# Filler matmuls moved ahead of a query sum and into the attention, in a one-core decoder layer on Trainium2

## The chip, the cores and the metric

The kernel runs on one core of a Trainium2 chip. The metric is the device time of one execution in microseconds (us). The engines have the names that the profile gives them: PE (TensorE) multiplies matrices, PEld is its loading of weights, DVE (VectorE), ACT (ScalarE) and POOL (GpSimd) work on tiles of 128 partitions, and SP (SyncE) here only issues DMA transfers.

## The reference

One layer of a hybrid decoder on 512 rows of 1024 numbers, all in float32:

```python
h = h + 0.5 * _swiglu(h, ffn1_norm, ffn1_w_gate, ffn1_w_up, ffn1_w_down)   # D_FF = 2816
h = h + _mixing(h, ...)
h = h + 0.5 * _swiglu(h, ffn2_norm, ffn2_w_gate, ffn2_w_up, ffn2_w_down)

def _mixing(x, ...):
    proj = _rmsnorm(x, mix_norm) @ w_in       # q, 6 x k/v, nsa_gate, ssm_u, gate_nsa, gate_ssm
    ...
    y_nsa = o_nsa @ w_nsa_proj    # 8 heads of 64: compressed, selected and window attention, gated and summed
    y_ssm = _s5_glu(...)          # a state space over 512 steps, GELU, then val * sigmoid(gate)
    merged = jax.nn.sigmoid(gate_nsa) * y_nsa + jax.nn.sigmoid(gate_ssm) * y_ssm
    return merged @ w_out
```

With 512 rows the selection and the window take in every earlier row, so these two branches are causal attention with keys of their own.

## The kernel before

Values lie transposed: a tile is 128 features by 512 rows. A product in float32 is made of three faster ones: both operands are split into a rounded high part and a remainder (`whi`, `wlo`; `xgh`, `xgl`), and `mm3` (L371 to L374) issues high by high, low by high and high by low. Weights come through SP's queue, in order, as slabs of 512 KB (eight blocks of 128 x 128, so 24 matmuls of 512 columns). There are five raw slabs; for each, ACT writes `whi` (L233) and DVE `wlo` (L234) two slabs ahead of use, into three slots. Other tiles come from one heap of 58 tiles of 256 KB (`H`), and the results of PE from eight banks (`PS`).

The order of the work on PE is written out by hand; the orders on the other engines come from a scheduler that follows it. The stages:

- The first feed-forward (until about 384 us). In its shadow the tables of the state space are prepared (`s5_prep`): 16 heap tiles, `vr`, `vi`, `er` and `ei` for four groups, which stay in the heap until each is used.
- The mixing's projections. `M1_ORDER` lists them: `u`, the compressed keys and values, the four state-space steps `S` (`s5_state`, first matmul L1058) and outputs `Y`, and the queries `q`. A query tile is squared by ACT (`qsq`, L1285), and `q_sums` (L1310) sums the squares on PE; the sums of tile t stand behind query tile t+1, and those of tile 3 stand alone. `q_scale` makes the scales `qs` of them. `cmp_k_norm` makes the compressed keys: ACT (`k2c`, `k2ct`), then DVE, which spreads them into the two `k2z` tiles (L1250, L1252), read by `c_scores` (`cs`, L1386).
- The attention: 64 units of a head, a branch and a quarter t of the rows. A unit is scored (`scores`, on DVE and ACT a softmax of (t+1) x 128 columns, tile `P`), turned by transposes two units later (`turn`, `pt`, L1457), and weighed (`weigh`). Between these PE does filler (`filler`): the projections of the 16 gate columns listed in `FILL` (`gs` and `gn`, tile `fx`) and the products of the state space's gated unit (`gl`). One filler step is one `mm3`, and a column is eight steps. `pad(n)` does n of them: PADA ahead of `q_sums(3)`, PADD between the two `c_scores`, then `STEP[min(i, 7)]` behind unit i's scores, four in each step of the tail, and what is left at the end.
- The gated sum: for each column a projection of the attention (`ns`) times its gate. The gates `gn` 4 to 7 are projected here, two ahead of each pair of `ns` (L1530 to L1537).
- The output projection (`wo`) and the second feed-forward (`fast_ffn`), which takes seven products P1 to P7 of halves instead of eight. The halves' sums are made by `side1` to `side3`: for four tiles DVE sums (L522, L523), ACT copies the high part (`xqh`, L492) and DVE takes the remainder (`xql`, L493). The third stage feeds P7 and P4. ACT also copies results out of banks (`mP`, L575). A down step adds finished banks (`dn`) to `xd`, fetched from `xhome` by SP (L614), on DVE (L618), and GpSimd stores them (L619).

The steps around the place of `side3` are P1, P2, down, P6, P5, down, P7, next P1, P4, P3.

Of the kernel before, what the change touches and what calls it, by code (L numbers as in the profile page):

```python
# [30 lines left out]
SPRI = 0  # L31
LAG = 2
PVLAG = 3
PADA, PADB, PADC, PADD = 4, 0, 0, 4
EX = (0, 2, 3, 4, 7)
NH = 58
PUMP = (4, 2, 3)
STEP = (1, 3, 2, 3, 4, 3, 4, 2)
WIDE = ("ffn1",)
WARM = 9  # L40
CUT = ((0, 256), (256, 512), (512, 1024))
# [89 lines left out]
def stream_plan():  # L131

    plan = []

    def blks(lst):
        assert len(lst) % 8 == 0
        for i in range(0, len(lst), 8):
            plan.append(("blk", lst[i:i + 8]))

    blks(ffn_blocks("ffn1", FF1_CHUNKS))  # L140
    cols = {"u": O_U, "kc": O_KC, "vc": O_VC, "q": O_Q, "gs": O_GS, "gn": O_GN}
    for kind in M1_ORDER + FILL:
        if kind[0] in cols:
            blks(proj(cols[kind[0]] + 128 * kind[1]))
        elif kind[0] == "gl":
            m = kind[1]
            blks([("ssm_glu_w", k * 128, D + m * 128) for k in range(4)]
                 + [("ssm_glu_w", k * 128, m * 128) for k in range(4)])
        elif kind[0] in SLAB_W:
            plan.append(kind)  # L150
    for m in range(0, KD, 2):
        if m > 2:
            blks(proj(O_GN + 128 * m))
            blks(proj(O_GN + 128 * (m + 1)))
        blks([("w_nsa_proj", k * 128, (m + a) * 128) for a in range(2) for k in range(4)])
    for m in range(KD):
        blks([("w_out", k * 128, m * 128) for k in range(KD)])
    return plan + fast_plan("ffn2")
# [4 lines left out]
for _n, _w in (("g1", 8), ("gm", 8), ("g2", 8), ("qn", 1), ("knc", 1), ("kns", 1), ("knw", 1),  # L163
# [7 lines left out]

M1_ORDER = [("u", 0), ("u", 1), ("u", 2), ("u", 3), ("kc", 0), ("tokk", 0), ("S", 0), ("tokk", 1),
            ("cmpk", 0), ("cmpk", 1), ("vc", 0), ("S", 1), ("tokv", 0), ("tokv", 1), ("S", 2), ("cmpk", 2),
            ("tokv", 2), ("q", 0), ("Y", 1), ("kt", 0), ("cmpv", 0), ("cmpk", 3), ("Y", 0), ("cmpv", 1),
            ("q", 1), ("S", 3), ("cmpv", 2), ("ck", 0), ("q", 2), ("Y", 2), ("cmpv", 3), ("cv", 0),
            ("ck", 1), ("q", 3), ("Y", 3)]
FILL = [("gs", 2), ("gs", 1), ("gs", 0), ("gl", 1), ("gs", 3), ("gl", 0), ("gs", 5), ("gl", 2), ("gs", 4),
        ("gl", 4), ("gl", 5), ("gl", 3), ("gs", 6), ("gl", 6), ("gs", 7), ("gn", 3), ("gn", 2), ("gn", 1),
        ("gl", 7), ("gn", 0)]


class Stream:
# [111 lines left out]
def build(ctx, tc, xT_in, wstream, small_in, out):  # L294
    nc = tc.nc
# [183 lines left out]
    def fast_ffn(p, gname, x, norm, xgh, xgl, home, nxt):  # L479
# [142 lines left out]
        for st in steps:  # L622
            if st[0] == "plain":
                f = st[1]
                ps = {nm: PS("gu") for nm in ("gate", "up")}
                for nm in ("gate", "up"):
                    for k in range(KD):
                        mm3(ps[nm], ws.blk(), xgh[k], xgl[k], k == 0, k == KD - 1)
                        if held and k == 0:
                            norm.b()  # L630
                            plain_end(0, held)
                            held = None
                            side1()
                    if f == 0 and nm == "gate":
                        norm.a()
                if f == 0:
                    held = ps
                    ws.fetch(p, 0)
                else:
                    plain_end(f, ps)  # L640
                ps = None
                if f == HEAD - 1:
                    for k in range(KD):
                        xgh[k] = xgl[k] = None
                    side2()
                    norm.R = None
            elif st[0] == "prod":
                product(*st[1:])
                if st[1:] == (0, "P2"):
                    side3()  # L650
                if st[1] == (FF // 128 - HEAD) // 2 - 1 and st[2] == "P3":
                    X.clear()
            else:
                down(st[1])


    s5 = {}

    def exp_acc(x, t, out):
        n, r, p, q = t  # L660
# [31 lines left out]
    def s5_prep():  # L692
# [140 lines left out]
        for hf in range(2):  # L833
# [19 lines left out]
            for T4 in (2 * hf, 2 * hf + 1):  # L853
                X = [H("xr"), H("xi")]
                for ri in range(2):
                    G.memset(X[ri], 0.0)
                    for g in range(2):
                        h = slice(64 * g, 64 * g + 64)
                        o4 = (T4 % 2) * 256
                        G.tensor_copy(  # L860
                            X[ri].rearrange("p (m g c) -> p m g c", g=2, c=16)[h, :, g, :],
                            Bk[ri][h, o4:o4 + 256].rearrange("p (m c) -> p m c", c=16))
                    yield
                for ri in range(2):
                    ps = PS("s5p")
                    for q in range(4):
                        PE.transpose(ps[:, q * 128:(q + 1) * 128], X[ri][:, q * 128:(q + 1) * 128], ident)
                    w = H("win")
                    S.activation(w, ps, AF.Copy)
                    s5[("vr", "vi")[ri]][T4] = w  # L870
                    yield
                ps = PS("s5k")
                for q in range(4):
                    n = T4 * 4 + q
                    PE.matmul(ps[:, q * 32:q * 32 + 32], X[0][:, q * 128:(q + 1) * 128], C0[:, n, :],
                              start=True, stop=False)
                    PE.matmul(ps[:, q * 32:q * 32 + 32], X[1][:, q * 128:(q + 1) * 128], C1[:, n, :],
                              start=False, stop=True)
                yield
                pv = ps[:, 0:128].rearrange("p (q c) -> p q c", q=4)  # L880
                i = 0
                for k in range(4):
                    for t in range(4 - k):
                        dst = s5["T"][32 * t:32 * t + 32, 4 * T4:4 * T4 + 4, 32 * (t + k):32 * (t + k) + 32]
                        srcp = pv[32 * (3 - k):32 * (3 - k) + 32]
                        if i % 2:
                            S.activation(dst, srcp, AF.Copy)
                        else:
                            V.tensor_copy(dst, srcp)
                        i += 1  # L890
                        if i % 5 == 0:
                            yield
                for q in range(4):
                    n = T4 * 4 + q
                    V.scalar_tensor_tensor(s5["T"][:, n, :], ident, smc("dd", n, n + 1), s5["T"][:, n, :],
                                           op0=ALU.mult, op1=ALU.add)
                    if q % 2:
                        yield

        for T4 in range(4):  # L900
# [6 lines left out]
            for k in range(7):  # L907
# [8 lines left out]
                G.tensor_tensor(u2[:, 1, :, :m], Er[:, :, 0:m], sw, op=ALU.mult)  # L916
                G.tensor_tensor(Ei[:, :, m:2 * m], u2[:, 0, :, :m], u2[:, 1, :, :m], op=ALU.subtract)
                yield
            s5["er"][T4], s5["ei"][T4] = er, ei

    gen = s5_prep()

# [77 lines left out]
        Up[t] = up  # L1000

    upend = []
    for t in range(4):
        ps = PS("pu")
        mm_proj(ps)
        upend.append(ps)
        if t == 0:
            nm.a()
        if t == 1:
            nm.b()  # L1010
            for i in range(2):
                u_evac(i, upend[i])
        if t > 1:
            u_evac(t, ps)
# [36 lines left out]


    def s5_state(t):
        pv = []
        for ri in range(2):
            ps = PS("s5v")
# [248 lines left out]
    def q_sums(t):  # L1305
# [3 lines left out]
        for tt in range(4):  # L1309
            PE.matmul(st_["pq2"][:, tt * 8 + 2 * t:tt * 8 + 2 * t + 2], sq[:, tt * 128:(tt + 1) * 128], bd2,  # L1310
                      start=True, stop=True)

    for kind, i in M1_ORDER[4:]:
        if kind in ("kc", "vc"):
            cmp_proj(kind)
# [14 lines left out]
        elif kind in ("cmpk", "cmpv"):  # L1330
            cmp_hidden(kind, i, blkc["kc" if kind == "cmpk" else "vc"])
            if i == 3:
                del blkc["kc" if kind == "cmpk" else "vc"]
        elif kind == "q":
            q_tile(i)
            if i:
                q_sums(i - 1)
        elif kind == "ck":
            (cmp_k_end, cmp_k_norm)[i]()
        elif kind == "cv":  # L1340
            cmp_v_mid()
    s5.clear()

    ms = [None] * KD

    tg, tn = {}, {}

    def filler():
        for kind, m in FILL:
# [14 lines left out]
            else:  # L1364
                px = PS("fx")
                for k in range(KD):
                    mm3(px, ws.blk(), xmh[k], xml[k], k == 0, k == KD - 1)
                    yield
                t1 = H("fs")
                V.tensor_tensor(t1, px, R, op=ALU.mult)  # L1370
                S.activation(t1, t1, AF.Tanh, scale=0.5)
                (tg if kind == "gs" else tn)[m] = t1

    fill = filler()

# [131 lines left out]
    for i in range(len(units) + LAG + PVLAG):  # L1507
        if i < len(units):
            scores(*units[i])
        pad(STEP[min(i, 7)] if i < len(units) else 4)  # L1510
        if i in extra:
            extra[i]()
        if LAG <= i < len(units) + LAG:
# [13 lines left out]

    mh, ml = [None] * KD, [None] * KD
    for m in range(0, KD, 2):
        if m > 2:  # L1530
            for a_ in range(2):
                ps = PS("gn")
                mm_proj(ps)
                t1 = H("gt")
                V.tensor_tensor(t1, ps, R, op=ALU.mult)
                S.activation(t1, t1, AF.Tanh, scale=0.5)
                tn[m + a_] = t1  # L1537
        for a_ in range(2):
            ps = PS("ns")
            for k in range(4):  # L1540
# [121 lines left out]
```

## Time and profile before

| what | value |
| --- | --- |
| three timed runs | 1146.85, 1148.93, 1151.59 us; median 1148.93 |
| profiled execution, own time | 1148.3 us |
| its span in the trace | 1146.6 us |
| mean granted TensorE clock | 0.994 |
| busy PE, DVE, ACT, POOL | 98%, 70%, 41%, 21% |

The span is the time from the first to the last instruction in the trace; the execution's own time has 1.7 us around it. The timed runs spread by 4.7 us. "Busy" counts instructions at work, and a matmul that runs at a lower clock is busy for longer. A row of a timeline has the start and the duration in us, the engine, the line, and in brackets the idle time ahead with the instruction that ended it.

### The profile page before, as it was taken

The numbers are of one execution on the slowest core, as the hardware profiler recorded it, in microseconds if no ns is written. First come the engines' busy times: TensorE is split into PE (matmuls) and PEld (weight loads), VectorE is DVE, ScalarE is ACT, GpSimd is POOL, SyncE is SP. The second block draws the span as 40 slices with busy tenths as digits, with TensorE's granted clock in tenths as the row PEclk, the third lists the DMA queues.
The fourth block names the chain that finished last, engine by engine and source line by source line (L and its number), as shares of the span: only waits on it lengthen the run. The fifth ranks groups of instructions, "written<-read, shape, count | busy, mean of one in ns | idle before, by whom it ended". The sixth has DMA issues, their size and how long they took to land.

```text
span 1146.6 us, 16136 instructions
## 1 busy us (share of the span) xinstructions
PE 1119.1 (98%) x6061; PEld 961.8 (84%) x6061; DVE 798.1 (70%) x1486; ACT 466.3 (41%) x748; POOL 236.4 (21%) x409
## 2 busy tenths in 40 slices
PE   9999999999999999989999999999989999999998
PEld 6888888888888898867878878888878999999986
DVE  6897555456556568589888986545886877768862
ACT  5332223232224321535666663333444444445530
POOL 2029540109608137020000000032001111110000
PEclk9999999999999999999999999999998999999999
DMA  8233232232324451643211112356245466555251
GB/s 297 80 100 103 93 105 79 92 92 74 111 92 139 147 163 57 222 140 99 73 45 48 56 56 92 132 202 198 90 149 178 154 202 198 188 179 143 102 184 74
DMA packets 52942, 144.16 MB, mean 126 GB/s; under 512 B 6400, under 2 KB 12800, under 8 KB 52864
## 3 DMA queue, kind: packets, MB, share of 16 engines
q1 hardware_dynamic: 48224, 127.79, 33.8%
q0 software_dynamic: 4496, 15.21, 4.8%
q8 instruction: 47, 0.77, 0.3%
q14 instruction: 31, 0.25, 0.1%
q10 hardware_dynamic: 144, 0.13, 0.0%
HBM read 123.19 MB, written 17.83 MB: 123 GB/s over the span
## 4 chain that ended last, share of the span: by engine, by line
PE 81%; issue 7%; DVE 6%; ACT 2%; POOL 2%; DMA 1%; SPq 0%; POOLq 0%; ACTq 0%
PE mA L569 9%; PE gu L373 8%; PE gu L374 8%; PE gu L372 8%; PE dn L372 7%; PE dn L373 7%; PE dn L374 7%; PE mC L569 4%; PE mB L569 2%; DMA wraw<-wstream 1%; DVE s5m L1075 1%; PE wo L374 1%; PE wo L372 1%; PE wo L373 1%; DVE wlo L234 1%
## 5 line engine op out<-in xcount | busy, mean ns | idle before, releaser
L233 ACT ACTIVATE whi<-wraw 128x1024 fp32r<-128x1024 f32 (+2 forms) x149 | 155.7, 1045 | 361.9 <-issue 105.6
L234 DVE TENSOR_TENSOR wlo<-wraw,whi 128x1024 fp32r<-128x1024 f32 (+2 forms) x149 | 187.8, 1261 | 75.0 <-ACT whi L233 74.4
L372 PE MATMUL gu<-xgh,whi 128*128 128x512 f32 x416 | 163.5, 393 | 0.5 <-ACT xgh L379 0.5
L373 PE MATMUL gu<-xgh,wlo 128*128 128x512 f32 x416 | 162.0, 389 | 0.8 <-DVE wlo L234 0.8
L372 PE MATMUL dn<-ah,whi 128*128 128x512 f32 x352 | 138.8, 394 | 6.7 <-DVE xd L618 6.7
L373 PE MATMUL dn<-ah,wlo 128*128 128x512 f32 x352 | 138.2, 393 | 0.0
L374 PE MATMUL dn<-al,whi 128*128 128x512 f32 x352 | 138.0, 392 | 0.0
L374 PE MATMUL gu<-xgl,whi 128*128 128x512 f32 x352 | 137.2, 390 | 0.1
L226 DVE TENSOR_TENSOR wlo<-wpair,whi 128x1024 fp32r<-128x1024 f32 x63 | 77.0, 1223 | 33.3 <-ACT whi L225 33.3
L372 PEld LDWEIGHTS gu<-xgh,whi 128*128 128x128 f32 x416 | 78.1, 188 | 17.8 <-ACT xgh L379 1.0
L373 PEld LDWEIGHTS gu<-xgh,wlo 128*128 128x128 f32 x416 | 78.1, 188 | 17.6 <-DVE wlo L234 1.1
L225 ACT ACTIVATE whi<-wpair 128x1024 fp32r<-128x1024 f32 x63 | 66.6, 1057 | 62.6 <-issue 28.7
L372 PEld LDWEIGHTS dn<-ah,whi 128*128 128x128 f32 x352 | 66.8, 190 | 20.5 <-DVE xd L618 7.2
L374 PEld LDWEIGHTS dn<-al,whi 128*128 128x128 f32 x352 | 66.8, 190 | 14.2
L374 PEld LDWEIGHTS gu<-xgl,whi 128*128 128x128 f32 x352 | 66.1, 188 | 14.2 <-DVE xgl L380 0.5
L373 PEld LDWEIGHTS dn<-ah,wlo 128*128 128x128 f32 x352 | 66.9, 190 | 13.2
L569 PE MATMUL mA<-xql,whi 128*128 128x256 f32 x216 | 61.1, 283 | 0.0
L569 PE MATMUL mA<-xqh,wlo 128*128 128x256 f32 x216 | 61.1, 283 | 0.0
L569 PE MATMUL mA<-xqh,whi 128*128 128x256 f32 x216 | 61.1, 283 | 0.0
L619 POOL DMA_DIRECT2D xhome<-xd x32 | 17.4, 545 | 193.3 <-DVE xd L618 191.4
L1442 ACT ACTIVATE P<-P,aw,qs 128x128 f32<-128x128 f32 (+1 forms) x64 | 41.6, 651 | 28.6 <-DVE aw L1441 28.1
L1494 POOL TENSOR_TENSOR ol<-of,oh 128x512 fp32r<-128x512 f32 x4 | 5.2, 1294 | 192.8 <-ACT oh L1493 192.8
(451 smaller groups left out, 2689.3 us busy)
## 6 DMA issues: line engine op xcount, KB each, us to landing
wraw<-wstream SPq DMA_DIRECT2D x151, 512.0 KB, 3.6
wpair<-wstream SPq DMA_DIRECT2D x36, 512.0 KB, 4.9
xd<-xhome SPq DMA_DIRECT2D x40, 256.0 KB, 4.9
xhome<-xd POOLq DMA_DIRECT2D x32, 256.0 KB, 5.3
wpair<-wstream POOLq DMA_DIRECT2D x9, 512.0 KB, 5.6
x<-xT SPq DMA_DIRECT2D x8, 256.0 KB, 5.6
xspill<-x SPq DMA_DIRECT2D x8, 256.0 KB, 2.4
gT<-gd SPq DMA_DIRECT2D x32, 64.0 KB, 2.0
```

Source lines behind the costliest of these rows:

```text
L225: nc.scalar.activation(hi, src, AF.Copy)
L226: nc.vector.tensor_tensor(lo, src, hi, op=ALU.subtract)
L233: nc.scalar.activation(hi[:, c], raw[:, c], AF.Copy)
L234: nc.vector.tensor_tensor(lo[:, c], raw[:, c], hi[:, c], op=ALU.subtract)
L372: PE.matmul(ps, hi, xh, start=start, stop=False)
L373: PE.matmul(ps, lo, xh, start=False, stop=False)
L374: PE.matmul(ps, hi, xl, start=False, stop=stop)
L569: PE.matmul(o, w[:, c], xx, start=first and n == 0, stop=last and n == 23, skip_group_check=True)
L619: nc.gpsimd.dma_start(home[d], xd)
L1075: V.tensor_tensor_scan(o[:, c], s5["rho"][:, n:n + 1].to_broadcast([128, 128]), i[:, c], 0.0, op0=ALU.mult, op1=ALU.add)
L1442: S.activation(p[:, :n], p[:, :n], AF.Exp, bias=w[:, 1:2], scale=qc, accum_out=w[:, 2:3])
L1494: G.tensor_tensor(ol[pr_], o, oh[pr_], op=ALU.subtract)
```

## The change

Five edits stand in the diff. (1) `PADA` goes from 4 to 12, and the entries of `FILL` are put in another order near its head. (2) The four gate columns `gn` 4 to 7 leave the gated sum and come to the end of `FILL`, which then has 192 steps instead of 160. From unit 7 on a unit has 2, 2, 2 or 3 steps by its t, instead of 2. (3) `side3` is called behind the first down step that follows P2, instead of directly behind P2. (4) The 16 state-space tables are written to DRAM by GpSimd when they are made, and fetched back by SP, four at a time: the first four ahead of the `u` projections, four more at the start of each `s5_state`. (5) The evacuation of a gate column becomes a function, and `M1_ORDER` is wrapped in other places; its entries are the same, and the new `gs` branch of its loop is never taken.

```diff
-PADA, PADB, PADC, PADD = 4, 0, 0, 4
+PADA, PADB, PADC, PADD = 12, 0, 0, 4
...
-STEP = (1, 3, 2, 3, 4, 3, 4, 2)
+STEP = (1, 3, 2, 3, 4, 3, 4)
+STEP_T = (2, 2, 2, 3)
...
-FILL = [("gs", 2), ("gs", 1), ("gs", 0), ("gl", 1), ("gs", 3), ("gl", 0), ("gs", 5), ("gl", 2), ("gs", 4),
+FILL = [("gs", 2), ("gs", 1), ("gs", 0), ("gs", 3), ("gl", 1), ("gs", 5), ("gl", 0), ("gl", 2), ("gs", 4),
         ("gl", 4), ("gl", 5), ("gl", 3), ("gs", 6), ("gl", 6), ("gs", 7), ("gn", 3), ("gn", 2), ("gn", 1),
-        ("gl", 7), ("gn", 0)]
+        ("gl", 7), ("gn", 0), ("gn", 4), ("gn", 5), ("gn", 6), ("gn", 7)]
...
                 product(*st[1:])
-                if st[1:] == (0, "P2"):
-                    side3()
...
             else:
                 down(st[1])
+                if X and ("P7", 0) not in X and ("P1", 0) in X and bank:
+                    side3()
...
+    s5d = {(nme, t): dp.tile([128, 512], F32, name=f"s5{nme}{t}") for nme in ("vr", "vi", "er", "ei") for t in range(4)}
+
+    def s5_fetch(t):
+
+        for nme in ("vr", "vi", "er", "ei"):
+            x = H(nme)
+            nc.sync.dma_start(x, s5d[nme, t])
+            s5[nme][t] = x
...
-                    s5[("vr", "vi")[ri]][T4] = w
+                    G.dma_start(s5d[("vr", "vi")[ri], T4], w)
...
-            s5["er"][T4], s5["ei"][T4] = er, ei
+            G.dma_start(s5d["er", T4], er)
+            G.dma_start(s5d["ei", T4], ei)
...
+    s5_fetch(0)
     for t in range(4):
         ps = PS("pu")
...
     def s5_state(t):
+        if t < 3:
+            s5_fetch(t + 1)
...
-        pad(STEP[min(i, 7)] if i < len(units) else 4)
+        pad(STEP[i] if i < len(STEP) else STEP_T[i % 4] if i < len(units) else 4)
...
     for m in range(0, KD, 2):
-        if m > 2:
-            for a_ in range(2):
-                ps = PS("gn")
-                mm_proj(ps)
-                t1 = H("gt")
-                V.tensor_tensor(t1, ps, R, op=ALU.mult)
-                S.activation(t1, t1, AF.Tanh, scale=0.5)
-                tn[m + a_] = t1
```

On ACT, ahead of the last query tile's square, before (`gh` and `ge` are steps of GELUs, `ge<-ph` that of the compressed keys and values):

```order
L233 ACTIVATE whi<-wraw 128x1024
L1107 ACTIVATE gh<-ge_4319 128x512
L975 ACTIVATE ge_4356<-ph 128x124
L1245 ACTIVATE k2c<-kcs,gk 64x62
L1246 ACTIVATE k2ct<-kcs,gk 64x62
L978 ACTIVATE ge_4356<-ge_4357 128x124
L1285 ACTIVATE qsq<-pq 128x512
L1290 ACTIVATE qh<-pq 64x512 x2
```

The same place of ACT now:

```order
L231 ACTIVATE whi<-wraw 128x1024
L1117 ACTIVATE gh<-ge_4383 128x512
L982 ACTIVATE ge_4420<-ph 128x124
L231 ACTIVATE whi<-wraw 128x1024
L1255 ACTIVATE k2c<-kcs,gk 64x62
L985 ACTIVATE ge_4420<-ge_4421 128x124
L1256 ACTIVATE k2ct<-kcs,gk 64x62
L1295 ACTIVATE qsq<-pq 128x512
L1300 ACTIVATE qh<-pq 64x512 x2
```

One more copy of a weight slab stands ahead of `k2c`, and `k2ct` stands behind the GELU's step.

On DVE, the third stage of input sums in the second feed-forward, before:

```order
L552 TENSOR_TENSOR u<-th,mc 128x256
L522 TENSOR_TENSOR xt<-xn 128x256
L523 SCALAR_TENSOR_TENSOR xt<-xt,xn 128x256
L226 TENSOR_TENSOR wlo<-wpair,whi 128x1024
...
L259 TENSOR_TENSOR wpair<-wpair 128x1024
L493 TENSOR_TENSOR xql<-xt,xqh 128x512
L522 TENSOR_TENSOR xt<-xn 128x256
L523 SCALAR_TENSOR_TENSOR xt<-xt,xn 128x256
L493 TENSOR_TENSOR xql<-xt,xqh 128x512
L618 SCALAR_TENSOR_TENSOR xd<-dn,xd 128x512 x4
```

The same stage on DVE now:

```order
L550 TENSOR_TENSOR u<-th,mc 128x256
L224 TENSOR_TENSOR wlo<-wpair,whi 128x1024
L520 TENSOR_TENSOR xt<-xn 128x256
L616 SCALAR_TENSOR_TENSOR xd<-dn,xd 128x512 x2
L521 SCALAR_TENSOR_TENSOR xt<-xt,xn 128x256
L616 SCALAR_TENSOR_TENSOR xd<-dn,xd 128x512 x2
...
L520 TENSOR_TENSOR xt<-xn 128x256
L521 SCALAR_TENSOR_TENSOR xt<-xt,xn 128x256
L257 TENSOR_TENSOR wpair<-wpair 128x1024
L491 TENSOR_TENSOR xql<-xt,xqh 128x512
```

The four additions stood behind the whole stage and now stand inside its first tile; the rest of the stage stands behind them, and the pair sum behind its fourth tile.

On ACT, the copies of that stage, before:

```order
L550 ACTIVATE th<-mc 128x256
L225 ACTIVATE whi<-wpair 128x1024
L492 ACTIVATE xqh<-xt 128x512
L225 ACTIVATE whi<-wpair 128x1024
L492 ACTIVATE xqh<-xt 128x512 x3
L575 ACTIVATE mP_7754<-mA 128x512
```

The same place of ACT now:

```order
L548 ACTIVATE th<-mc 128x256
L223 ACTIVATE whi<-wpair 128x1024 x2
L490 ACTIVATE xqh<-xt 128x512 x2
L223 ACTIVATE whi<-wpair 128x1024
L490 ACTIVATE xqh<-xt 128x512 x2
L573 ACTIVATE mP_7818<-mA 128x512
```

A third weight copy now stands between the second and the third of the four copies, and the copy of the first product's bank still stands behind all four.

More of the change, by code (lines that the diff above doesn't have):

```diff
@@ L151, in stream_plan @@
     for m in range(0, KD, 2):
-        if m > 2:
-            blks(proj(O_GN + 128 * m))
-            blks(proj(O_GN + 128 * (m + 1)))
         blks([("w_nsa_proj", k * 128, (m + a) * 128) for a in range(2) for k in range(4)])
@@ L173 @@
             ("cmpk", 0), ("cmpk", 1), ("vc", 0), ("S", 1), ("tokv", 0), ("tokv", 1), ("S", 2), ("cmpk", 2),
-            ("tokv", 2), ("q", 0), ("Y", 1), ("kt", 0), ("cmpv", 0), ("cmpk", 3), ("Y", 0), ("cmpv", 1),
-            ("q", 1), ("S", 3), ("cmpv", 2), ("ck", 0), ("q", 2), ("Y", 2), ("cmpv", 3), ("cv", 0),
-            ("ck", 1), ("q", 3), ("Y", 3)]
-FILL = [("gs", 2), ("gs", 1), ("gs", 0), ("gl", 1), ("gs", 3), ("gl", 0), ("gs", 5), ("gl", 2), ("gs", 4),
[3 rows of a table added]
+FILL = [("gs", 2), ("gs", 1), ("gs", 0), ("gs", 3), ("gl", 1), ("gs", 5), ("gl", 0), ("gl", 2), ("gs", 4),
         ("gl", 4), ("gl", 5), ("gl", 3), ("gs", 6), ("gl", 6), ("gs", 7), ("gn", 3), ("gn", 2), ("gn", 1),
-        ("gl", 7), ("gn", 0)]
+        ("gl", 7), ("gn", 0), ("gn", 4), ("gn", 5), ("gn", 6), ("gn", 7)]
 class Stream:
@@ L1311, in q_sums, with branch_gate @@
                       start=True, stop=True)
+    tg, tn = {}, {}
+    def branch_gate(kind, m, px):
+        t1 = H("fs")
+        V.tensor_tensor(t1, px, R, op=ALU.mult)
+        S.activation(t1, t1, AF.Tanh, scale=0.5)
+        (tg if kind == "gs" else tn)[m] = t1
     for kind, i in M1_ORDER[4:]:
@@ L1337, in build @@
                 q_sums(i - 1)
+        elif kind == "gs":
+            ps = PS("fx")
+            mm_proj(ps)
+            branch_gate(kind, i, ps)
+            ps = None
         elif kind == "ck":
@@ L1344, in build @@
     ms = [None] * KD
-    tg, tn = {}, {}
     def filler():
@@ L1368, in filler @@
                     yield
-                t1 = H("fs")
-                V.tensor_tensor(t1, px, R, op=ALU.mult)
-                S.activation(t1, t1, AF.Tanh, scale=0.5)
-                (tg if kind == "gs" else tn)[m] = t1
+                branch_gate(kind, m, px)
     fill = filler()
@@ L1529, in build @@
     for m in range(0, KD, 2):
-        if m > 2:
-            for a_ in range(2):
-                ps = PS("gn")
-                mm_proj(ps)
-                t1 = H("gt")
-                V.tensor_tensor(t1, ps, R, op=ALU.mult)
-                S.activation(t1, t1, AF.Tanh, scale=0.5)
-                tn[m + a_] = t1
         for a_ in range(2):
```

3 rows, old and new, of the table M1_ORDER are left out of this document.

## The prediction, made before the changed kernel was run

> **What bounds the kernel now.** I read the head of the page first: how long the span is, and how much of it TensorE is busy.
>
> ```profile
> span 1146.6 us, 16136 instructions
> PE 1119.1 (98%) x6061; PEld 961.8 (84%) x6061; DVE 798.1 (70%) x1486; ACT 466.3 (41%) x748; POOL 236.4 (21%) x409
> ```
>
> TensorE (PE) is idle for 27.5 us of 1146.6, and the change takes no matmul away: it only reorders them. So a gain can come only from idle time on PE, and from time in which PE runs at a lower granted clock. PE's view of waits says where it is idle (columns: us in total, times, longest).
>
> ```profile
> PE dn L372 <- DVE xd L618: 6.7, 1, 6.7
> PE pq L1310 <- ACT qsq L1285: 5.2, 2, 3.6
> PE pt L1457 <- DVE P L1444: 3.0, 4, 1.6
> PE kt L1198 <- ACT gate L1187: 3.0, 2, 2.5
> ```
>
> Three of these four lie where the change works: the down step of the second feed-forward, the last query sum, and the attention. The timeline of PE around the query sum comes next (start, duration).
>
> ```profile
> 507.20 0.39 PE L373 MATMUL fx<-xgh,wlo 128*128 128x512 f32 x1
> 507.43 0.39 PE L374 MATMUL fx<-xgl,whi 128*128 128x512 f32 x1
> 511.40 1.05 PE L1310 MATMUL pq<-bd,qsq 128*128 128x2 f32 x8 [3.59 <-ACT qsq L1285]
> 512.32 0.60 PE L1386 MATMUL cs<-qh,k2z 128*128 128x512 f32 x1
> 515.70 0.51 PE L372 MATMUL fx<-xgh,whi 128*128 128x512 f32 x1
> ```
>
> Matmuls of 512 columns start 0.23 us apart before the wait. After it the eight of the compressed scores `cs` take 512.32 to 515.70, 0.42 us each. The windows (length, busy PE, PEld, DVE, ACT, POOL, then granted clock, DMA share, GB/s) say why.
>
> ```profile
> 511.00:515.00 4.00, 3.60 (x15) 3.01 (x16) 3.75 (x20) 1.54 (x4) 0.00 (x0) 0.69 0.71 222
> 459.10:462.00 2.90, 2.41 (x21) 2.18 (x21) 1.89 (x6) 2.09 (x7) 0.47 (x1) 1.00 0.57 181
> 861.50:867.40 5.90, 5.88 (x14) 4.67 (x15) 1.76 (x3) 0.00 (x0) 2.18 (x4) 0.50 0.48 178
> ```
>
> After the 3.59 us wait the granted clock is 0.69, after the 6.74 us one (third row) 0.50, and after the 2.5 us one (second row) still 1.00. So a long wait costs twice: itself, and a stretch at half speed behind it.
>
> **Part 1, the query sum.** PADA goes from 4 to 12: eight steps of three matmuls, 24 x 0.2275 = 5.46 us, now stand ahead of `q_sums(3)`. They come out of the attention, so they are free where PE stood idle. What PE waits for is a chain on ACT, and for `cs` one on DVE.
>
> ```profile
> 506.75 1.04 ACT L233 ACTIVATE whi<-wraw 128x1024 fp32r<-128x1024 f32 x1
> 508.37 0.33 ACT L1245 ACTIVATE k2c<-kcs,gk 64x62 fp32r<-64x62 f32 x1
> 510.56 0.31 ACT L978 ACTIVATE ge<-ge 128x124 f32<-128x124 f32 x1 [1.49 <-DVE ge L977]
> 510.77 0.58 ACT L1285 ACTIVATE qsq<-pq 128x512 f32<-128x512 f32 x1
> 510.95 0.48 DVE L1250 MEMSET k2z<- 128x512 f32 x1 [0.17 <-issue]
> 513.06 0.44 DVE L1252 CAST k2z<-k2c 128x31 fp32r<-128x31 f32 x4
> 518.75 0.19 DVE L1302 SCALAR_TENSOR_TENSOR qs<-qn__4506,nr_m 128x32 f32<-128x32 f32 x1
> ```
>
> Four steps end at 507.66; twelve end at 507.66 + 5.46 = 513.1. The steps are not free of side effects: a new column's weights are needed earlier, so one more `whi` copy now stands on ACT ahead of k2c, ge, k2ct and qsq (in the order). It needs the slot of the first column, free when eight steps have ended, at 510.4. So qsq ends at 510.4 + 1.04 + 0.33 + 0.31 + 0.33 + 0.58 = 513.0: the 3.59 us wait is gone, by 0.1 us. But DVE's k2c comes behind ACT's k2ct, 2 us later than before, and behind it the memsets and casts of `k2z` that `cs` reads: ready at 514.5 to 515.2, against 514.0, when the query sum ends (513.1 + 0.9, its start-to-next in the rows above). New wait 0.5 to 1.3 us, too short for the clock by the rows above. `cs` then ends near 516.8 (8 x 0.2275 behind 515.0) instead of 515.70, with 5.46 us more of the filler behind it: gain 5.46 - 1.1 = 4.4. Queued behind the waiting DVE work is the scale `qs` (518.75 before, about 2 to 3 us later now), which the first units' exponentials need. PE gets there 1 us later, so some 1 us of this comes back as a wait. Net **-3.5** (bounds: -5.5 if nothing comes back; 0 if the entry's delay and a longer `cs` wait eat it all).
>
> **Part 2, the attention.** From unit 7 on, the filler steps behind a unit's scores go from 2 to 2, 2, 2, 3 (three where t is 3, the longest), and four more columns (192 steps, not 160) feed them.
>
> ```profile
> 560.00:600.00 40.00, 37.55 (x200) 30.50 (x199) 33.63 (x108) 25.93 (x61) 1.29 (x1) 1.00 0.16 53
> 600.00:640.00 40.00, 39.70 (x211) 32.59 (x210) 36.63 (x115) 26.79 (x63) 1.29 (x1) 1.00 0.16 53
> 640.00:680.00 40.00, 39.33 (x210) 32.32 (x209) 34.87 (x110) 25.39 (x61) 1.30 (x1) 1.00 0.15 53
> L234 DVE TENSOR_TENSOR wlo<-wraw,whi 128x1024 fp32r<-128x1024 f32 x18 | 22.2, 1234 | 1.9 <-ACT whi L233 1.4
> L1370 DVE TENSOR_TENSOR fs<-fx,R 128x512 f32<-128x512 f32 x11 | 7.5, 686 | 2.5 <-PE fx L374 1.6 <-PE pt L1457 1.0
> ```
>
> PE is idle 2.45 + 0.30 + 0.67 = 3.4 us in these three windows. DVE is 84, 92 and 87% busy. A column brings PE 5.46 us and DVE 1.23 + 0.69 = 1.92 us, 35% of it, so four columns (21.9 against 7.7 us) thin DVE out relative to PE, and the softmax chain that `pt` waits for gets 0.68 us more time per fourth unit. The same 21.9 us of matmuls leaves the stage behind. I take three quarters of the idle time, **-2.5** (bounds: -3.4 if all goes, +1 if the bunched DVE work behind a column's end holds up `pt`; nearer to the first, since the two windows with 0.30 and 0.67 us show that this pace can be kept).
>
> **Part 3, the stage behind.** Without the gate columns between them the four `ns` slabs of eight blocks stand back to back, 24 x 0.2275 = 5.46 us each.
>
> ```profile
> 700.00:760.00 60.00, 60.00 (x266) 49.73 (x265) 35.68 (x45) 22.14 (x30) 4.23 (x5) 1.00 0.41 140
> ```
>
> PE never waits here today, and DVE is 59% busy. Per slab DVE will have 1.23 + 6 x 0.69 = 5.4 us, just under PE's 5.46, so its last products come about 4 us into the first output column, which reads them in order and needs the last ones then. **+0.5** (bounds 0, and 1.5 for two evictions of 0.69).
>
> **Part 4, the third stage of input sums.** `side3` moves behind the following down step. In the next rows: the down step with its stall, product P7 that follows, the fetch of `xd`, the additions that free the banks, and the stage's own work on DVE and ACT.
>
> ```profile
> 853.23 0.40 PE L372 MATMUL dn<-ah,whi 128*128 128x512 f32 x1
> 861.52 0.80 PE L372 MATMUL dn<-ah,whi 128*128 128x512 f32 x1 [6.74 <-DVE xd L618]
> 868.52 0.28 PE L569 MATMUL mA<-xqh,whi 128*128 128x256 f32 x1
> 850.49 1.82 SPq L614 DMA_DIRECT2D xd<-xhome  x4
> xd<-xhome SPq DMA_DIRECT2D x40, 256.0 KB, 4.9
> 851.09 0.42 DVE L523 SCALAR_TENSOR_TENSOR xt<-xt,xn 128x256 f32<-128x256 f32 x1
> 856.99 1.22 DVE L259 TENSOR_TENSOR wpair<-wpair 128x1024 f32<-128x1024 f32 x1
> 859.06 0.42 DVE L523 SCALAR_TENSOR_TENSOR xt<-xt,xn 128x256 f32<-128x256 f32 x1
> 860.79 2.48 DVE L618 SCALAR_TENSOR_TENSOR xd<-dn,xd 128x512 f32<-128x512 f32 x4
> 860.05 0.58 ACT L575 ACTIVATE mP<-mA 128x512 f32<-128x512 f32 x1
> ```
>
> Today the four additions stand behind the whole stage on DVE. In the new order they stand behind its first instruction and the fetch: 850.49 + 4.9 = 855.4 instead of 860.79. The down step stalls from 854.8 to about 856.3, 1.5 us, and ends at 853.23 + 5.46 + 1.7 = 860.4 at full clock, 8.1 us ahead of the 868.52 at which P7 starts now. But P7 needs that stage, which is now the late one. From its first second half to the fourth, 851.09 to 859.48, DVE took 8.4 us; 1.2 of these are the pair sum that now stands behind, and 0.6 were waits: 6.6. So the fourth input is summed at 855.4 + 2.48 + 6.6 = 864.5; ACT's copy of it (0.6) and then `mP` (0.58), which stands behind it on ACT and holds P7's bank, end at 865.7. PE idles from 860.4 to 865.7, 5.3 us. Against 868.52 that is 2.8 us earlier. The 5.3 us lie between the waits of 3.59 and 6.74 that cost clock, so a slow stretch follows them, worth 4.0 x 0.31 = 1.2 us by the 0.69 row and 5.9 x 0.5 = 2.9 us by the 0.50 row; I take 2.3, nearer to the longer wait: net **-0.5** (bounds: -8.1 if P7 finds its inputs ready at 860.4; +3 if ACT's copies queue behind a weight copy that waits for its slot).
>
> The Trainium skill's page "TensorE: Matmul & The Clock Gate", section "Part 1: The HAM clock gate", says that an idle window of about 3.4 us halves the clock, that about 3.4 us of work restores it, and that the window runs free of the kernel. This case's rows agree (2.5 us: no loss; 3.59 and 6.74 us: loss). By that rule the 5.3 us wait of P7 halves the clock again, which speaks against this part, and its recovery of 3.4 us would cost an estimated 1.7 us, part 4 then being -1.1.
>
> **Part 5, the state-space tables.** Sixteen tiles of 256 KB go to DRAM and come back.
>
> ```profile
> L619 POOL DMA_DIRECT2D xhome<-xd x32 | 17.4, 545 | 193.3 <-DVE xd L618 191.4
> 415.65 31.63 SPq L206 DMA_DIRECT2D wraw<-wstream  x7
> 441.20 1.95 PE L1058 MATMUL s5v<-up,win 128*128 128x128 f32 x16
> ```
>
> The writes are 16 GpSimd issues of 0.55 us, 8.7 us during the first feed-forward, where no PE wait names POOL but one of 1.2 us at the start. The fetches add 16 issues to SP's queue, four at a time, one state step ahead of use: next to the 4.9 us of a 256 KB transfer, a state step is over 10 us away (7 slabs in 31.63 us, 4.5 us each). **0** (bounds 0 and +2; a queued fetch holds back the weights behind it).
>
> **Sum.** -3.5 - 2.5 + 0.5 - 0.5 + 0 = -6.0 on the profiled execution's 1148.3 us: 1142.3. The median of the runs, 1148.93, lies 0.6 above that execution: **1142.9 us**. About 0.5%, 5.7 us, is what a measurement can tell from no change: faster is below 1143.2, slower above 1154.7.
>
> **The rivals.**
> *The stall of the second feed-forward really goes.* If ACT takes `mP` ahead of the last copies, or P7 starts on its first inputs, its wait falls under 2.5 us and the clock stays: part 4 is -8.1 instead of -0.5, 1135.3 us. For it: P7 reads its inputs one by one. Against it: the order on ACT has `mP` behind all four copies. Chance 0.18.
>
> *The filler buys nothing.* The entry to the attention is bound by DVE and ACT (3.75 of 4.00 us busy in the 511 window on DVE), so what the query sum no longer waits for, `cs` and the first `pt` do; and the attention keeps its waits, as DVE sets its pace. Parts 1 and 2 are then -2 together instead of -6: 1146.9 us. For it: the DVE rows of part 1. Against: the window from 640 shows PE idle for 0.67 us with DVE at 87%. This is also the case that the change doesn't do what it says. Chance 0.27.
>
> *A fetch of the tables blocks the weights.* SP issues in order. If a fetch finds no free tile of the heap, every weight slab behind it waits. Five raw slabs at 4.5 us cover about 18 us; beyond that each microsecond is PE's. A fetch that waits 30 us costs 12: 1142.9 + 12 = 1154.9 us, slower than before from a wait of 24 us on. For it: 16 tiles taken in four lots in the stage with the most tiles in use. Against: those 16 tiles were held through the whole stage before, so each lot asks for less than was held. Chance 0.09.
>
> **How the numbers follow.** Forecast 0.46, rivals 0.18, 0.27, 0.09. The forecast's own range, from its unknown costs, is 1139 to 1147, 0.6 of it below 1143.2. Faster: 0.28 + 0.18 + 0.05 of the second rival = 0.51. Slower: 0.07 of the third rival. The rest, 0.42, is no change that can be told. The range 1134.0 to 1149.5 leaves out the third rival and a tenth at the ends of the others.
>
> **What would show it.** Right: no wait of `pq` on qsq but one of about 1 us at `cs`, and the clock at 1.00 from 511 to 517; `pt` waits of 1 to 2 us in sum; a stall of some 1.5 us in the down step and one of some 5 us at P7's first matmul, with a clock near 0.5 behind it; no new wait on weights between 400 and 480. Wrong: P7 without a wait (first rival), `pt` or `cs` waits of over 4 us in all (second), any wait of PE on `wlo` in the state-space steps (third).

## The result, and the profile after

The changed kernel took 1166.69 us (median of four runs, 1165.52 to 1167.87) against 1150.26 us for the kernel before beside it: 1.0136 of its time, 95% interval 1.0120 to 1.0152. It is about 16 us slower, where 1142.9 us and a gain were forecast. One execution of the changed kernel with 59 tiles (1598.22 us) and one of the kernel before beside it (2546.56 us) ran in a slow state and are left out of the medians, ranges and ratios below. The page of the changed kernel:

```profile
span 1165.7 us, 16232 instructions
PE 1128.5 (97%) x6061; PEld 968.5 (83%) x6061; DVE 802.5 (69%) x1486; ACT 466.2 (40%) x748; POOL 240.3 (21%) x425
```

PE has the same 6061 matmuls; it is idle for 37.2 us instead of 27.5, and its busy time has grown by 9.4 us, which is matmuls at a lower clock. Its view of waits (us in total, times, longest; the rows of `warm`, `gu` and `kc`, 1.2 us and less, are left out) says where the idle time went:

```profile
PE pt L1475 <- DVE P L1462: 16.6, 8, 5.6
PE mA L567 <- ACT mP L573: 5.0, 1, 5.0
PE kt L1208 <- ACT gate L1197: 3.9, 1, 3.9
PE pq L371 <- DVE wlo L232: 2.3, 1, 2.3
PE pq L1320 <- ACT qsq L1295: 1.6, 1, 1.6
PE cs L1404 <- DVE k2z L1262: 0.9, 1, 0.9
PE dn L370 <- DVE xd L616: 0.4, 2, 0.3
```

The 6.7 us on `xd` and the 3.6 us on `qsq` are gone, as forecast, and the waits of P7 (5.0) and of `cs` (0.9) are there, as forecast. The attention's wait on `P` was to shrink from 3.0 us and has grown to 16.6. That of `pq` on `wlo` is new, and that of `kt` on the gates, 3.0 us before, is 3.9. Laid along the timeline by the first matmul of each stage, with the filler moved across a border taken out (the 32 steps of three matmuls, 3 x 0.2275 = 0.6825 us each, that left the gated sum: 8 of them now stand ahead of the first score, 24 behind it), the 19.1 us between the two spans fall so:

| from, to | before | after | difference, filler taken out |
| --- | --- | --- | --- |
| start, first `u` projection | 378.75 | 379.32 | +0.6 |
| that, first score | 520.68 | 528.12 | 148.80 - 5.46 - 141.93 = +1.4 |
| that, first `ns` | 698.39 | 742.06 | 213.94 - 16.38 - 177.71 = +19.9 |
| that, first product `mA` | 836.26 | 858.16 | 116.10 + 21.84 - 137.87 = +0.1 |
| that, end of span | 1146.6 | 1165.7 | 307.5 - 310.3 = -2.8 |

Nearly all of it is the attention. The second row can't be read to a few us: the kernel before with only `side3` moved, which is the same up to there, took 147.2 us where the row has 141.9 (the last section says why). The whole stage from the first score to the first `ns`, before and then changed (length, busy PE, PEld, DVE, ACT, POOL, granted clock, DMA share, GB/s):

```profile
520.68:698.39 177.71, 173.94 (x914) 142.69 (x913) 152.87 (x465) 108.59 (x246) 3.88 (x3) 1.00 0.18 62
```

```profile
528.12:742.06 213.94, 197.28 (x986) 160.91 (x985) 161.79 (x473) 114.72 (x255) 5.54 (x4) 0.96 0.18 60
```

PE is idle for 16.7 us of this stage instead of 3.8. The rest of the 19.9 us, 7.0 us, goes with the lower granted clock. Two windows of the stage in the changed kernel:

```profile
560.00:600.00 40.00, 32.37 (x146) 25.67 (x144) 24.86 (x74) 16.90 (x39) 0.00 (x0) 0.87 0.11 36
600.00:640.00 40.00, 32.71 (x160) 26.09 (x159) 29.35 (x88) 20.85 (x47) 1.64 (x1) 0.91 0.15 53
```

DVE is busy for 62% and 73%, less than before (84% and 92%), while PE waits for it. So it isn't short of time: it waits too. The tile `P` of the changed kernel between 560 and 640 us, as DVE sees it, and then two of DVE's waits and the longest wait of PE:

```profile
its engine sat idle before it (us, times) until:
  PE pt L1475: 6.3, 7
  POOL ol L1512: 1.2, 1
  PE sc L1453: 0.7, 1
who waited for it (us, times):
  PE pt L1475: 14.9, 7
```

```profile
607.63 0.29 DVE L1456 CUSTOM_DVE_ANT_0 P<-sc,causal 128x128 f32<-128x128 f32 x1 [1.15 <-POOL ol L1512]
618.48 0.29 DVE L1456 CUSTOM_DVE_ANT_0 P<-sc,causal 128x128 f32<-128x128 f32 x1 [2.57 <-PE pt L1475]
609.58 0.45 PE L1475 MATMUL pt<-ident,P 128*128 128x128 f32 x1 [5.58 <-DVE P L1462]
```

A unit's first addition reads the scores `sc` and writes a new tile `P`. It waits seven times for transposes `pt`, which read the `P` of an earlier unit: what it lacks is not its input but a tile to write to. At 607.63 us it is released by GpSimd's `ol` instead, which does not make its input either: by the kernel's text it reads another tile of the heap (`of`), which comes free then. The transposes of that unit stand behind it at 609.58. Before, between the same times, it never waited for `pt`:

```profile
its engine sat idle before it (us, times) until:
  POOL ol L1494: 1.3, 1
  PE sc L1435: 0.2, 1
who waited for it (us, times):
  PE pt L1457: 2.8, 3
```

In the order of DVE the same thing shows without any time: I count, for each unit's scores, how many units they stand ahead of the transposes taken over by DVE. Before it is two or three from unit 2 on. In the changed kernel it is none or one for eleven of the units 9 to 28, and two or three again behind these.

### The profile page after: what moved, and what is told of

It reads as the page before. It is cut to its first block, busy times and chain, and to the rows that moved or that the text cites. A ratio compares the mean times of both kernels' runs of the same rounds, so it can differ in the third digit from the quotient of the medians.

```text
span 1165.7 us, 16232 instructions
## 1 busy us (share of the span) xinstructions
PE 1128.5 (97%) x6061; PEld 968.5 (83%) x6061; DVE 802.5 (69%) x1486; ACT 466.2 (40%) x748; POOL 240.3 (21%) x425
## 4 chain that ended last, share of the span: by engine, by line
PE 45%; issue 9%; DVE 2%; ACT 0%; DMA 0%; POOL 0%; SPq 0%; ACTq 0%; POOLq 0%
PE mA L567 9%; PE mC L567 4%; PE dn L370 3%; PE dn L371 3%; PE dn L372 3%; PE mB L567 2%; PE fx L370 2%; PE fx L372 2%; PE fx L371 2%; PE gu L370 1%; PE gu L372 1%; PE wo L371 1%; PE wo L370 1%; PE gu L371 1%; PE wo L372 1%
## 5 line engine op out<-in xcount | busy, mean ns | idle before, releaser
L232 DVE TENSOR_TENSOR wlo<-wraw,whi 128x1024 fp32r<-128x1024 f32 (+2 forms) x149 | 185.4, 1245 | 74.1 <-ACT whi L231 73.9
```

What stands on the lines that cost most here:

```text
L232: nc.vector.tensor_tensor(lo[:, c], raw[:, c], hi[:, c], op=ALU.subtract)
```

## The experiments

Theory **heap**: the filler comes earlier (eight steps at the query sum, two gate columns ahead of gated products in the list, and the third steps), and each gate column leaves a tile of the heap behind until it is used; with 58 tiles the scores then lack one. Rival **load**: the moved filler gives DVE and ACT more work than fits beside the softmax. For the mixing, theory **order**: the fetches make the scheduler put DVE's work in another order; rival **transfer**: they are hidden. All times are medians beside runs of the kernel before on the same chip.

### More tiles, and one less

```diff
-NRAW = 5
+NRAW = 4
...
-NH = 58
+NH = 60
```

> The changed kernel with 60 heap tiles instead of 58, paid for with 4 raw weight slabs instead of 5. Theory heap: in the attention the score tile P of units 9 to 30 finds no free tile, so the additions of scores on DVE stand behind the transposes that free one; with 60 tiles they stand two units ahead again, PE's waits of pt on P fall from 16.6 us to under 5 us, the clock stays at 1.00 from 560 to 640 us, and the time falls by 14 to 18 us, to 1149 to 1153 us. Theory load: the moved filler brings DVE and ACT more work than they can do beside the softmax; the number of tiles changes nothing, 1165 to 1169 us, or more if four raw slabs are too few.

Measured: 1150.10 us, 1.0001 of before (0.9982 to 1.0021).

```diff
-NH = 58
+NH = 59
```

> The changed kernel with 59 heap tiles, nothing else. Theory heap: one tile more mends part of it (of the 13 units whose scores stand less than two ahead, about 8 are left, most of them by one): waits of pt on P between 5 and 11 us, 1155 to 1162 us. Theory load: no change, 1165 to 1169 us.

Measured: 1154.56 us, 1.0035 (1.0017 to 1.0053), with waits at the lower end of what theory heap gave. And in the kernel before, one tile less:

```diff
-NH = 58
+NH = 57
```

> The kernel before with 57 heap tiles instead of 58, no other change, so with its own filler. Theory heap: the kernel before has just enough tiles; one less puts the scores of units 10 to 26 behind the transposes as in the changed kernel, waits of pt on P rise from 3.0 to 12 us or more, and the time rises by 10 to 18 us, to 1159 to 1168 us. Theory load: the filler is that of before, so 1147 to 1152 us.

Measured: 1165.39 us, 1.0126 (1.0096 to 1.0156). In these three PE waits for `P` in the transposes as follows (first 60 tiles, then 59, then the kernel before with 57; of the last also the window):

```profile
PE pt L1475 <- DVE P L1462: 0.6, 2, 0.3
```

```profile
PE pt L1475 <- DVE P L1462: 5.1, 4, 3.4
```

```profile
PE pt L1457 <- DVE P L1444: 13.4, 13, 2.7
560.00:600.00 40.00, 29.73 (x143) 22.85 (x142) 27.50 (x83) 19.40 (x45) 1.28 (x1) 0.96 0.12 40
```

| kernel | units from 9 on with scores less than two ahead | wait of `pt` on `P` | first score to first `ns`, filler taken out |
| --- | --- | --- | --- |
| before | 0 | 3.0 us | 177.7 us |
| before, 57 tiles | 9 | 13.4 us | 191.3 us |
| changed | 11 | 16.6 us | 197.6 us |
| changed, 59 tiles | 6 | 5.1 us | 181.8 us |
| changed, 60 tiles, 4 slabs | 1 | 0.6 us | 176.1 us |

Load falls: with the filler as changed and two tiles more, the attention is 1.6 us faster than before; with the filler as before and one tile less, it is 13.6 us slower. The kernel before has about as many tiles as it needs. The run with 60 tiles also has a raw slab less; the run with 59, which has all five, shows that the tiles do it.

### The filler as before

The changed kernel with PADA 4, the old list ahead of the four new entries, and two steps per unit:

```diff
-PADA, PADB, PADC, PADD = 12, 0, 0, 4
+PADA, PADB, PADC, PADD = 4, 0, 0, 4
...
-FILL = [("gs", 2), ("gs", 1), ("gs", 0), ("gs", 3), ("gl", 1), ("gs", 5), ("gl", 0), ("gl", 2), ("gs", 4),
+FILL = [("gs", 2), ("gs", 1), ("gs", 0), ("gl", 1), ("gs", 3), ("gl", 0), ("gs", 5), ("gl", 2), ("gs", 4),
...
-        pad(STEP[i] if i < len(STEP) else STEP_T[i % 4] if i < len(units) else 4)
+        pad(STEP[i] if i < len(STEP) else 2 if i < len(units) else 4)
```

> The changed kernel with its filler placed as before: four steps ahead of the query sum, the entries in the old order, two steps per unit; the four gate columns stay in the filler and run behind the last unit; spill and third stage as changed, 58 tiles. Theory heap: only the filler's being early fills the heap, so the attention keeps the pace of before, and what is left is the spill's 5 to 6 us less the third stage's 0 to 2: 1152 to 1156 us. Theory load: the moved columns themselves make it slow: 1160 us or more.

Measured: 1152.38 us, 1.0025 (1.0012 to 1.0038), with waits of `pt` on `P` as before (3.0 us):

```profile
PE pt L1475 <- DVE P L1462: 3.1, 4, 1.6
```

So the four gate columns may stand at the end of the filler, where they run behind the last unit; what fills the heap is that the filler comes early. Which of the three early moves does it with 58 tiles (the eight steps, the order of the list or the third steps) was not run apart.

### The tables

The changed kernel without the stores and the fetches:

```diff
...
-                    G.dma_start(s5d[("vr", "vi")[ri], T4], w)
+                    s5[("vr", "vi")[ri]][T4] = w
...
-            G.dma_start(s5d["er", T4], er)
-            G.dma_start(s5d["ei", T4], ei)
+            s5["er"][T4], s5["ei"][T4] = er, ei
...
-    s5_fetch(0)
...
-        if t < 3:
-            s5_fetch(t + 1)
```

> The changed kernel with the state-space tables kept in the heap as before (no stores, no fetches). Theory order: the fetches make the scheduler put DVE's evacuations of kce, which wait for PE, ahead of the key norm, which holds up kd, the scan and a weight split; without them PE's waits on wlo (2.3 us) and on the gates (3.9 instead of 3.0 us) go back, and the time falls by 4 to 6 us, to 1161 to 1163 us, the attention staying slow. Theory transfer: what held PE there comes from the moved filler, or the fetches cost nothing: 1165 to 1169 us.

Measured: 1161.73 us, 1.0100 (1.0066 to 1.0135), 4 to 5 us under the changed kernel, with an interval that overlaps the changed kernel's; the wait on `wlo` is gone, the gates' is 2.5 us, the 15.4 us in the attention stay. The spill alone, in the kernel before (the same lines the other way round):

> The kernel before with only the spill of the 16 state-space tables and their fetches. Theory order: DVE's evacuations of kce stand ahead of the key norm, as in the changed kernel, a wait of PE on wlo of 2 to 2.5 us and one on the gates of 3.5 to 4 us with a lower clock behind it appear, and the time rises by 3 to 6 us, to 1153 to 1156 us. Theory transfer: the fetches are hidden and cost nothing by themselves: 1148 to 1152 us.

Measured: 1155.57 us, 1.0053 (1.0034 to 1.0072): 6 us slower, and this is clear of the noise. The wait on `wlo` is there; the longer one at the gates, which was expected too, is not (2.8 us in all, 3.0 before).

```profile
PE pq L373 <- DVE wlo L234: 2.3, 1, 2.3
```

It isn't late transfers that cost. In the changed kernel DVE, POOL and PE stand so (second and third fence the same kernel, POOL and PE):

```profile
430.92 0.42 DVE L1038 TENSOR_TENSOR kce<-pc,R 64x256 f32<-64x256 f32 x1 [3.78 <-PE pc L372]
438.21 0.17 DVE L1157 TENSOR_TENSOR ksum<-kn,nr_m 128x16 f32<-128x16 f32 x1
449.82 1.22 DVE L232 TENSOR_TENSOR wlo<-wraw,whi 128x1024 fp32r<-128x1024 f32 x1
```

```profile
433.35 3.54 POOL L1046 TENSOR_TENSOR bq<-kce,sm 128x496 f32<-128x496 f32 x2 [4.99 <-DVE kce L1038]
438.53 4.04 POOL L1164 TENSOR_TENSOR kd<-kraw,ksum 128x512 f32<-128x512 f32 x4 [1.64 <-DVE ksum L1157]
```

```profile
451.10 0.50 PE L371 MATMUL pq<-xgh,wlo 128*128 128x512 f32 x1 [2.28 <-DVE wlo L232]
```

and before:

```profile
430.16 0.17 DVE L1147 TENSOR_TENSOR ksum<-kn,nr_m 128x16 f32<-128x16 f32 x1
445.24 1.22 DVE L234 TENSOR_TENSOR wlo<-wraw,whi 128x1024 fp32r<-128x1024 f32 x1
```

Before, DVE made the keys' norm (`ksum`) while PE worked on `pc`, and took `pc` over behind it. Now the takeover stands ahead, DVE waits 3.78 us in its place, the norm is 8.05 us late, POOL's `kd` behind it too (438.53 against 430.48), and the scan that follows on DVE, 4.6 us late (443.83 against 439.22), holds the weight split that PE waits for. Nothing there waits for a fetched table, and the fetches land in 4.3 to 4.9 us (medians). The spill alone has the same rows (`kce` with a wait of 3.78 us, `ksum` at 437.83). So the spill changes the order; whether by its transfers or by the tiles that it frees is not shown.

### The third stage, and twelve steps, alone

The kernel before with only `side3` moved, as in the diff of the change:

> The kernel before with only the third stage of input sums moved behind the down step. Theory trade: the 6.7 us stall of the down step goes, a wait of about 5 us of P7 on the copy mP takes its place, with a stretch at a low clock behind it; from mA's later start to the end of the span 2 to 4 us are won, as in the changed kernel: 1146 to 1149 us beside 1150. Theory full: the stall was worth 8 us and something else in the changed kernel took it back: 1141 to 1144 us.

Measured: 1150.97 us, 1.0008 (0.9993 to 1.0022): no change that can be told, and outside what either theory gave. PE waits 5.1 us for `mP` and 0.8 for `xd`. From `mA` to the end the five profiles with the old place took 308.9 to 310.3 us (mean 309.4), the nine with the new one 307.3 to 309.7 (mean 308.3). The difference is 1.1 us, less than the timed runs can tell.

The kernel before with twelve steps and 59 tiles:

```diff
-PADA, PADB, PADC, PADD = 4, 0, 0, 4
+PADA, PADB, PADC, PADD = 12, 0, 0, 4
-NH = 58
+NH = 59
```

> The kernel before with twelve filler steps ahead of the last query sum and 59 heap tiles, so that the scores of the attention stay two units ahead of the transposes. Theory gain: the wait of pq on qsq of 3.6 us and the half clock behind it go, a wait of about 1 us at cs stays, and the attention keeps its pace: 3 to 5 us faster than before, 1145 to 1148 us. Theory entry: the later DVE work at the start of the attention takes the gain back: 1149 to 1152 us.

Measured: 1148.55 us, 0.9988 (0.9974 to 1.0002): not told from no change, and between what the two theories gave. With the third stage too:

> The kernel before with twelve filler steps ahead of the last query sum, 59 heap tiles and the moved third stage; tables, filler entries and gate columns as before. Theory heap, order and trade together: the gains of the two moves add and nothing is paid in the attention or the mixing: 5 to 8 us faster, 1142 to 1146 us. Theory entry: only the third stage's part is left, 1147 to 1149 us.

Measured: 1149.90 us, 0.9999 (0.9985 to 1.0013), so the gains did not add: a miss. Both profiles show 2.2 us of idle PE at 340 to 384 us (`dn` waiting for the split of its activations) and 1.7 us more between the first `ns` and `mA`. The control, the kernel before with 59 tiles and nothing else:

> The kernel before with 59 heap tiles, nothing else: the control for the runs with 59. If the tile alone moves the order in the first feed-forward and in the gated sum, as the runs with 59 tiles and kept tables show (2.2 us idle at 340 to 384 us, 1.6 us between the gated sum and the second feed-forward), it is 2 to 4 us slower, 1151 to 1154 us; if that came from the moved steps, 1148 to 1151 us.

Measured: 1147.42 us, 0.9980 (0.9967 to 0.9993): faster, the other way than expected, and without these two losses. So the tile alone does not cause them, and the changed kernel, which has the twelve steps too, has no such idle time with 58 tiles, with 59, or with 59 and the tables kept (below); where these losses come from stays open.

### Both mends together

The changed kernel with the tables kept, 60 tiles and 4 raw slabs:

> The changed kernel with the tables kept in the heap, and with 60 heap tiles and 4 raw weight slabs: the mends for the attention and for the mixing together. Theory heap and order, two separate causes: their gains add, so about 5 us below the run with 60 tiles alone, 1143 to 1147 us, under both kernels. Theory overlap: the mixing's waits are only moved or the order changes elsewhere: 1148 to 1152 us.

Measured: 1145.19 us, 0.9946 (0.9925 to 0.9967). With 59 tiles, 5 slabs and two steps per unit:

> The changed kernel with the tables kept, 59 heap tiles, and two filler steps per unit from unit 7 on (the left-over columns run behind the last unit). Its scores stand two or three units ahead of the transposes throughout. Theory heap and order: no wait of pt on P over 2 us, 1144 to 1149 us. Theory overlap: 1149 to 1153 us, since one more tile also changes the order in the first feed-forward, where 59 tiles showed two waits of 1 us.

Measured: 1146.05 us, 0.9960 (0.9945 to 0.9975). Both are faster than before and than the changed kernel. How much of this is the moves' own is less clear: the kernel before with 59 tiles has 0.9980 without any of them, so with 59 tiles they are worth some 0.2% (here without the third steps), and the intervals overlap. The forecast had 6 us for parts 1 to 4 together. The windows of the first (60 tiles) show the attention full:

```profile
560.00:600.00 40.00, 39.33 (x208) 32.18 (x207) 33.87 (x110) 25.59 (x60) 1.29 (x1) 1.00 0.18 60
600.00:640.00 40.00, 40.00 (x209) 32.96 (x209) 35.80 (x106) 25.91 (x59) 1.30 (x1) 1.00 0.16 53
```

PE's idle time in these 80 us is 0.7 us, where it was 2.75 before: the filler can bring 2 us here when the tiles are there.

## Why the prediction was wrong

**The step that failed** is part 2, -2.5 us, with bounds of -3.4 and +1. It costed a column by its time on PE and DVE and said that more filler thins DVE out. The last windows, with PE full, have DVE busy for 69.7 of 80 us instead of 70.3, so that reading of DVE holds. What the part left out is what a column holds: a tile. The heap of 58 was named in the text only for the fetches, and as relief. The measured term is +19.9 us in place of -2.5: 16.7 - 3.8 = 12.9 us more idle PE and 7.0 us at a lower clock, by the two rows of the stage. The order of DVE, which was at hand, shows it: scores behind transposes in eleven units. I read that order at the query sum and at the third stage, and not in the attention.

**Part 5**, 0 with bounds 0 and +2, was wrong in size: 4 to 6 us by the runs with and without the spill. Of the ways it could cost, the forecast named only a transfer that comes late or blocks SP. What costs is a changed order on DVE, an engine that the edit doesn't name.

**Part 1** was right on the wait and its successor: `q_sums` waits for nothing, `cs` 0.9 us where 0.5 to 1.3 was forecast.

```profile
517.80 1.05 PE L1320 MATMUL pq<-bd,qsq 128*128 128x2 f32 x8
519.76 0.50 PE L1404 MATMUL cs<-qh,k2z 128*128 128x512 f32 x1 [0.91 <-DVE k2z L1262]
517.00:523.00 6.00, 5.09 (x23) 3.96 (x22) 5.65 (x24) 2.38 (x5) 0.00 (x0) 0.85 0.60 179
521.21:524.62 3.41, 3.41 (x9) 2.66 (x9) 3.17 (x11) 1.52 (x3) 0.00 (x0) 0.50 0.85 237
```

But the clock was not at 1.00 behind it: it was half from 521.21 to 524.62, with PE at work throughout, so 3.41 x 0.5 = 1.7 us were lost, which the forecast had put at nothing. The price of -3.5 us is not confirmed: with 59 tiles, twelve steps (0.9988) are no faster than four (0.9980). Without the 3.8 us that the kernel with twelve steps lost in two other places (2.16 and 1.67) it would come near -3, but that is argued and not shown.

**Part 3** (+0.5) measured +0.1. **Part 4** was right in mechanism: the stall became a wait of P7 on `mP` of 5.03 us (5.3 forecast), with a lower clock behind it; what was left of the stall is 0.4 us (1.5 forecast).

```profile
886.85 0.58 PE L567 MATMUL mA<-xqh,whi 128*128 128x256 f32 x1 [5.03 <-ACT mP L573]
886.85:892.85 6.00, 6.00 (x39) 6.00 (x40) 1.23 (x2) 1.51 (x3) 0.00 (x0) 0.75 0.30 115
```

The clock cost 6.0 x 0.25 = 1.5 us here, 2.3 were charged; the gain over many profiles is 1.1 us, 0.5 was forecast, and the timed runs of this part alone show none.

**The rivals.** The one on the slower side had the right direction, and the sign named for it came, a wait of PE on `wlo`; but it came by another mechanism, since no fetch of the tables waited for more than 0.2 us in SP's queue. "The filler buys nothing" had the place, and its sign came too, waits of `pt` and `cs` of over 4 us; but it gave 1146.9 us, and its reason, that DVE sets the pace, is what the runs with 57 and 60 tiles refute. That these signs came was luck: neither rival had the scores short of a tile.

## What to carry to other kernels

Work moved forward holds its results longer: before costing the engines, count the buffers that it keeps, and look in the new order for instructions that now stand behind the reader that frees one. Where a scheduler makes the orders of the other engines, look at the whole of each order for in-order waits on another engine, also far from the edit. A stage with waits that don't grow under load, on an engine that is less busy than before, is short of space, not of time.

## What the runs showed of the hardware

The same wait of 2.5 us, in the same place of nearly the same program (the transposes `kt` behind the gates), left the clock alone in three of nine profiles that have it, halved it for 3.4 us in two, and for 10.2 to 13.7 us in four. The kernel before, then the kernel before with `side3` moved, which is the same up to there:

```profile
459.08 1.09 PE L1198 MATMUL kt<-ident,kd 128*128 128x128 f32 x8 [2.50 <-ACT gate L1187]
460.00:476.00 16.00, 15.09 (x110) 13.84 (x108) 8.38 (x13) 9.27 (x16) 0.00 (x0) 1.00 0.68 217
```

```profile
459.84 1.41 PE L1198 MATMUL kt<-ident,kd 128*128 128x128 f32 x8 [2.48 <-ACT gate L1187]
460.00:476.00 16.00, 15.83 (x85) 15.43 (x84) 8.91 (x14) 9.96 (x19) 0.33 (x1) 0.57 0.69 215
```

16 us at 0.57 are 6.9 us of lost work, about the spread of the runs of before beside the first experiments (1146.8 to 1154.3 us). The wait of 0.91 us at `cs` is no safer: the clock was half behind it in the changed kernel and stayed at 1.00 from 517 to 527 us in the kernel before with twelve steps and 59 tiles. In all 14 profiles the record of the clock has only full and half, and but for the end of the span a stretch at half lasts 3.41 us or two, three or four times that; the 0.69 of the prediction is an average over such a stretch (512.52 to 515.94 us) and full clock beside it. So the statement in the prediction that waits of up to 2.5 us are too short to cost clock holds for one execution and not for the program, and a span from a single profile is no measure of an edit worth less than that. The Trainium skill's page "TensorE: Matmul & The Clock Gate", section "Part 1: The HAM clock gate", says that the window runs free of the kernel, which agrees with a loss that comes and goes; its idle window of about 3.4 us does not by itself explain a loss at 2.48 us.
